# Hymba encoder layer: Hyena's projection begun ahead of the attention loop, and four small tables loaded by GpSimd at the start

## The chip, the cores and the metric

The kernel runs on one core of one Trainium2 chip. The metric is the device time of one execution in microseconds (us). Each core has a tensor engine (PE, with its weight loads shown apart as PEld), a vector engine (DVE), a scalar engine (ACT), GpSimd (POOL) and SyncE (SP), which issues most DMAs here. Each engine runs its instructions in the order of its own queue; between engines and DMAs they wait on semaphores.

## What is computed

One encoder layer on x of 2048 tokens by 1024 features, float32. A root-mean-square norm and one input projection give q (8 heads of 64), k and v (2 heads of 64), and u (3 x 512 columns). Half of the mixer is grouped-query attention over all tokens, half is a Hyena operator on u: a convolution of width 3, then two rounds of a long convolution by FFT with filters from a small network, each gated. Then output projection, residual, MLP, residual, norm. Cut to the lines that matter here:

```
proj = rms_norm(x, norm1_g) @ w_in
q, k, v, u = split(proj)                  # 512, 128, 128, 1536 columns
att = softmax(q k^T / 8) v                # after norm and rotation of q and k
v, x1, x2 = split(short_conv(u, conv_w, conv_b))      # 3 taps per column
z = v; for n, gate in ((0, x1), (1, x2)): z = gate * (fft_long_conv(z, taps_f[n]) + skip_d[n] * z)
taps = (h @ w4) * exp(-t * abs(deltas))   # h from a small network on time features; taps_f is their FFT
mix = concat(rms_norm(att), rms_norm(z)); h = x + mix @ w_out; MLP; norm
```

## The kernel before

All matrices stay float32: an operand is split into a high and a low part, and `mm3` (lines 162 to 166) makes a product of three matmuls. Stage 1, `qkv_proj`, takes 16 tiles of 128 tokens: transposes of the normed x (`tp`), 8 x 3 matmuls each for two groups of columns (`qkv`), norm and rotation on DVE and POOL, then transposes of the result (`tq`), a cast on ACT into `qs` (three buffers) and stores by SP of `q_d`, `k_d` and `v_d`. The split input weights of q, k and v (`wh`, `wl`) stay in SBUF for the whole stage. The normed, split x is stored too (`aT_d`), for u. `filter_hidden` runs beside it (`sx`, `hc`).

Attention has 32 units (16 query blocks for each of the two key heads) of 16 steps. A step makes one score peak (`sc` on PE, `top` on DVE), one block of weights (`st`, two matmuls, then the exponential `p` on ACT), sums of p on POOL (`sum`), and products with v (`o`, later `of`). Peaks run 22 steps ahead of the weights (`AHEAD`). At each step one yield of side work is taken: first 16 yields of `taps_ahead`, with an empty one after each (`spaced`), so 8 taps, then one yield of taps for every six of `u_proj` (`mixed`), and what remains runs behind the loop. Taps are `ft` (two matmuls), `taps` on DVE and a store to `taps_d`.

`u_proj` computes u and the short convolution: four blocks of 512 tokens by 12 column tiles of 128. For the first block, a column tile's weights are loaded (`uraw`), split on ACT and DVE in eight pieces (`uw`, lines 361 and 363), and stored (`uw_d`) for the other blocks, the split of the next tile running beside the matmuls (`uo`, 24 a tile) of this one. Its first yields are the nine of the first weight tile; each column tile has ten more. The order in attention and stage 1 is found by the framework's scheduler from the dependencies and the order of the code; each engine's queue is then fixed. From `filter_dft` on (`fs` on line 1465) the order is that of the code. SP's DMAs have eight semaphore lanes in turn, so that a DMA waits for the one eight places ahead to land.

The small tables are the convolution's weights and bias `cw` and `cb` (4608 and 1536 elements), the filters' decays `dl` (2048) and the skip weights `skip` (1024). They are loaded one 4-byte element at a time, by SP, at the start of attention: lines 336 and 339 in `u_proj`, 1278 and 1286 in `taps_ahead`.

Of the kernel before, what the change touches and what calls it, by code (L numbers as in the profile page):

```python
# [11 lines left out]
F32 = mybir.dt.float32  # L12
F32R = mybir.dt.float32r
# [32 lines left out]
def setup(tc, ctx, a):  # L46
# [10 lines left out]
    aligned(k.cpool, 64)  # L57
# [114 lines left out]
def qkv_proj(k, pa, ps, side):  # L172
# [10 lines left out]
    nc.gpsimd.memset(unit[:, 0:1], 1.0)  # L183
    W = QW + 2 * NKV * HD
    wh = pa.tile([P, ND, W], F32R, name="wh", bufs=1)
    wl = pa.tile([P, ND, W], F32R, name="wl", bufs=1)

    def load_w(c0, c1):
        for d in range(ND):
            raw = pa.tile([P, c1 - c0], F32, name=f"wraw{c0}", bufs=2)  # L190
# [5 lines left out]
    def load_x(t):  # L196
        xt = pa.tile([P, DM], F32, name="xt", bufs=2)
        nc.sync.dma_start(out=xt[:], in_=x[t * P:(t + 1) * P, :])
        return xt
# [99 lines left out]
    for i in range(-1 - XL, NT + FL):  # L299
# [21 lines left out]
        if 0 <= i < NT:  # L321
            okv = project(*aT.pop(i), QW, 256)
        if 0 <= i - 1 < NT:
            hl[i - 1] = twice(norm_rope(i - 1, *yz.pop(i - 1)))
        if 0 <= i < NT:
            yz[i] = taken(i, oq.pop(i), okv)
    pump(side, 10 ** 6)


def u_proj(k, pu, ps):  # L330
# [7 lines left out]
    cb = pu.tile([P, nct], F32, name="cb", bufs=1)  # L338
    nc.sync.dma_start(out=cb[:], in_=a["hy_conv_b"][0].rearrange("(c p) -> p c", p=P),
                      allow_slow_non_contiguous=True)  # L340
    edge = pu.tile([P, nct, 2], F32, name="edge", bufs=1)
    aligned(pu, 64)

    def load_a(b, d):
        t = pu.tile([P, 2, H], F32R, name="aT", bufs=ND)
# [3 lines left out]
    def load_w(b, ct):  # L349

        w = pu.tile([P, 2, ND, P], F32R, name="uw", bufs=2)
# [4 lines left out]
        raw = pu.tile([P, ND, P], F32, name="uraw", bufs=2)  # L356
# [16 lines left out]

    nw, rest = load_w(0, 0)
    aT = [load_a(0, d) for d in range(ND)]
    for _ in rest:
        yield
    for b in range(NB):
        last = b == NB - 1
        for ct in range(nct):  # L380
# [64 lines left out]
def attention(k, a1, ps, side):  # L445
# [94 lines left out]
    pump(side, START)  # L540
    for step in range(-AHEAD, total + FIN + 1):
# [34 lines left out]
START = 0  # L576
# [690 lines left out]
def filter_taps(k, f1, ps):  # L1267
# [535 lines left out]
```

## Time and profile before

| what | us |
|---|---|
| median of 3 runs | 3157.62 (3154.59 to 3162.08) |
| the profiled execution | 3165.88 |
| its span | 3164.1, mean granted clock 0.975 |
| stage 1, to its last transposes | 0 to 227.5 |
| attention, first `st` to the last `of` | 267.5 to 1219.6 |
| first `fs` behind attention | 1236.6 |

The rows that the prediction rests on follow the change. In them L with a number is a line of the kernel before; SPq, ACTq and the like are an engine's queue, where its DMAs are issued; a row of a timeline with a count stands for several instructions in a row.

### The profile page before, as it was taken

How to read it: one execution, taken by the hardware profiler on the slowest of the kernel's cores; microseconds unless marked ns; L12 is line 12 of the kernel's file. 1: busy time of each engine (PE TensorE's matmuls, PEld its weight loads, DVE VectorE, ACT ScalarE, POOL GpSimd, SP SyncE). 2: the span in 40 equal slices, each digit the busy share in tenths (PEclk: the TensorE clock that was granted, in tenths of full speed). 3: DMA queues.
4: the chain of work that ended last, by engine and by line, in shares of the span. 5: the costliest groups of instructions: out<-in, count | busy, mean ns of one | idle time of the engine just before them, and what ended most of it. 6: DMA issues, size and time to landing. Idle time of an engine off the chain costs nothing.

```text
span 3164.1 us, 40514 instructions
## 1 busy us (share of the span) xinstructions
PE 2989.5 (94%) x13400; PEld 2251.3 (71%) x13400; DVE 2048.8 (65%) x3153; ACT 1423.2 (45%) x2626; POOL 1715.1 (54%) x1399
## 2 busy tenths in 40 slices
PE   8978999999998998999999988999999989999998
PEld 6755666666665666676667766888788778888887
DVE  7987777666665554777465567778877535454455
ACT  7866655555553444444444563333433223223333
POOL 3434777778776876244555326777876635250010
PEclk9988999999998999999999998999999999999999
DMA  7758334324334425776656784445644395333454
GB/s 226 221 155 232 115 125 159 110 95 151 125 107 108 140 80 163 263 248 218 186 172 197 253 290 157 156 154 174 204 158 151 121 316 171 133 115 129 146 181 153
DMA packets 482462, 534.45 MB, mean 169 GB/s; under 512 B 49604, under 2 KB 344004, under 8 KB 475212
## 3 DMA queue, kind: packets, MB, share of 16 engines
q1 hardware_dynamic: 464540, 513.16, 50.4%
q0 software_dynamic: 4480, 14.68, 1.3%
q10 hardware_dynamic: 13232, 4.01, 0.6%
q8 instruction: 107, 1.75, 0.2%
q14 instruction: 103, 0.84, 0.1%
HBM read 326.22 MB, written 198.19 MB: 166 GB/s over the span
## 4 chain that ended last, share of the span: by engine, by line
PE 75%; DVE 5%; DMA 5%; issue 3%; POOL 3%; ACT 2%; SPq 1%; ACTq 0%; POOLq 0%; DVEq 0%
PE o L502 7%; PE y L164 6%; PE y L165 6%; PE y L166 6%; PE g L166 5%; PE g L165 5%; PE g L164 5%; PE st L481 4%; PE X L1435 4%; PE st L482 3%; PE sc L461 3%; PE uo L164 3%; PE uo L165 2%; PE uo L166 2%; PE b L1565 2%
## 5 line engine op out<-in xcount | busy, mean ns | idle before, releaser
L489 POOL TENSOR_TENSOR sum<-sum,p 128x512 f32<-128x512 f32 x416 | 552.9, 1329 | 125.3 <-ACT p L484 98.9
L464 DVE TENSOR_REDUCE top<-sc 128x1 f32<-128x512 f32 x512 | 347.4, 687 | 255.4 <-PE sc L461 252.3
L484 ACT ACTIVATE p<-st 128x512 f32<-128x512 f32 x512 | 303.2, 597 | 317.6 <-PE st L482 299.9
L164 PE MATMUL g<-mh,wop 128*128 128x512 f32 x896 | 350.5, 391 | 17.9 <-ACT wop L914 17.6
L165 PE MATMUL g<-ml,wop 128*128 128x512 f32 x896 | 350.6, 391 | 2.8 <-DVE ml L925 2.8
L166 PE MATMUL g<-mh,wop 128*128 128x512 f32 x896 | 350.4, 391 | 2.4 <-DVE wop L915 2.4
L164 PE MATMUL y<-bh,ah 128*128 128x512 f32 x768 | 299.8, 391 | 15.5 <-ACT bh L1082 15.5
L1091 DVE TENSOR_TENSOR ah<-ar,ah 128x1024 fp32r<-128x1024 f32 x111 | 148.9, 1342 | 235.2 <-ACT ah L1090 232.9
L165 PE MATMUL y<-bh,ah 128*128 128x512 f32 x768 | 299.7, 390 | 0.0
L166 PE MATMUL y<-bh,ah 128*128 128x512 f32 x768 | 299.7, 390 | 0.0
L1090 ACT CAST ah<-ar 128x1024 fp32r<-128x1024 f32 x111 | 117.0, 1054 | 347.8 <-PE y L166 343.0
L502 PE MATMUL o<-p,vt 128*64 128x512 f32 x1024 | 234.9, 598 | 0.0
L461 PE MATMUL sc<-kt,q 128*128 128x512 f32 x512 | 208.0, 410 | 15.0 <-DVE top L464 11.9
L481 PE MATMUL st<-q,kt 128*128 128x512 f32 x512 | 215.0, 420 | 1.6 <-ACT p L484 1.4
L164 PEld LDWEIGHTS g<-mh,wop 128*128 128x128 f32 x896 | 169.2, 189 | 54.2 <-ACT wop L914 18.0
L482 PE MATMUL st<-q,kt 128*128 128x512 f32 x512 | 203.8, 398 | 0.0
L165 PEld LDWEIGHTS g<-ml,wop 128*128 128x128 f32 x896 | 169.0, 189 | 38.9 <-DVE ml L925 3.9
L166 PEld LDWEIGHTS g<-mh,wop 128*128 128x128 f32 x896 | 169.1, 189 | 38.4 <-DVE wop L915 3.5
L914 ACT CAST wop<-ws 128x512 fp32r<-128x512 f32 x128 | 79.1, 621 | 223.5 <-PE g L166 192.1
L164 PEld LDWEIGHTS y<-bh,ah 128*128 128x128 f32 x768 | 144.7, 189 | 46.2 <-ACT bh L1082 15.9
L166 PEld LDWEIGHTS y<-bh,ah 128*128 128x128 f32 x768 | 144.7, 188 | 30.3
L165 PEld LDWEIGHTS y<-bh,ah 128*128 128x128 f32 x768 | 144.7, 188 | 30.2 <-DVE bh L1083 0.2
(306 smaller groups left out, 7054.6 us busy)
## 6 DMA issues: line engine op xcount, KB each, us to landing
ar<-H_d SPq DMA_DIRECT2D x111, 512.0 KB, 3.8
uw<-uw_d SPq DMA_DIRECT2D x36, 1024.0 KB, 5.0
w1raw<-in_w_mlp_in SPq DMA_DIRECT2D x64, 512.0 KB, 4.2
H_d<-r SPq DMA_DIRECT2D x96, 256.0 KB, 2.2
H_d<-s SPq DMA_DIRECT2D x96, 256.0 KB, 2.0
F_d<-F SPq DMA_DIRECT2D x34, 512.0 KB, 3.2
F<-F_d SPq DMA_DIRECT2D x34, 512.0 KB, 4.6
aT<-aT_d SPq DMA_DIRECT2D x32, 512.0 KB, 6.6
```

The source lines that it names most:

```text
L164: mm(out, l_hi, r_hi, start=start, stop=False)
L165: mm(out, l_hi, r_lo, start=False, stop=False)
L166: mm(out, l_lo, r_hi, start=False, stop=stop)
L461: nc.tensor.matmul(s[:], u.q[:, h], kt[u.kv, b][0][:], start=True, stop=True)
L464: nc.vector.tensor_reduce(out=u.top[:, h, b:b + 1], in_=s[:], axis=AX.X, op=ALU.max, negate=True)
L481: nc.tensor.matmul(s[:], lo[:, c], u.q2[:].rearrange("p h t -> p (h t)"), start=True, stop=False)
L482: nc.tensor.matmul(s[:], hi[:, c], u.q[:].rearrange("p h t -> p (h t)"), start=False, stop=True)
L484: nc.scalar.activation(out=p[:], in_=s[:], func=AF.Exp)
L489: nc.gpsimd.tensor_add(out=u.sum[:], in0=u.p0[:] if j == 1 else u.sum[:], in1=p[:])
L502: nc.tensor.matmul(u.o[cols], vt[j // 8][:, j % 8, u.kv], p[:], start=j < 2, stop=j > 13)
L1091: nc.vector.tensor_sub(out=h[:, 1], in0=raw[:], in1=f32(h[:, 0]))
L1435: k.nc.tensor.matmul(d[:, ri], t[:, m], Af[:, 2 * j + at], start=True, stop=True)
```

## The change

The weights `wh` and `wl` get a pool of their own, which ends behind the last tile's matmuls. In its memory `u_proj` is begun there: its first weight tile and the eight `aT` loads of its first block are issued. When attention begins, 49 yields of u are taken ahead of all else: nine for the first weight tile, and four column tiles. The peak of step 12 of the first unit may not be issued before the last of these matmuls. The four small tables are loaded by GpSimd at the kernel's start, behind the memsets of `unit`, and kept for the whole kernel. Stage 1's pools move to the other side of the memory.

```diff
@@ setup: the four small tables get places in the constant pool
     k.norm = k.cpool.tile([P, 4], F32, name="norm")
-    aligned(k.cpool, 64)
+    k.cw = k.cpool.tile([P, 3, 12], F32, name="cw")
+    k.cb = k.cpool.tile([P, 12], F32, name="cb")
+    k.dl = k.cpool.tile([P, 16], F32, name="dl")
+    k.skip = k.cpool.tile([P, 2, 4], F32, name="skip")
+    aligned(k.cpool, 256)
@@ mm3
-    mm(out, l_lo, r_hi, start=False, stop=stop)
+    return mm(out, l_lo, r_hi, start=False, stop=stop)
@@ qkv_proj: the tables' loads, the weights' own pool, and its early end
-def qkv_proj(k, pa, ps, side):
+def qkv_proj(k, pa, ps, side, after):
     nc.gpsimd.memset(unit[:, 0:1], 1.0)
+    nc.gpsimd.dma_start(out=k.cw[:], in_=a["hy_conv_w"][0].rearrange("w (c p) -> p w c", p=P),
+                        allow_slow_non_contiguous=True)
...
+    pw_pool = sbuf(k, "pw")
+    pw = pw_pool.__enter__()
+    wh = pw.tile([P, ND, W], F32R, name="wh", bufs=1)
+    wl = pw.tile([P, ND, W], F32R, name="wl", bufs=1)
...
             okv = project(*aT.pop(i), QW, 256)
+            if i == NT - 1:
+                pw_pool.__exit__(None, None, None)
+                next(after())
@@ u_proj
-def u_proj(k, pu, ps):
+def u_proj(k, pu):
-    cw = pu.tile([P, 3, nct], F32, name="cw", bufs=1)
-    nc.sync.dma_start(out=cw[:], in_=a["hy_conv_w"][0].rearrange("w (c p) -> p w c", p=P),
-                      allow_slow_non_contiguous=True)
...
+    cw, cb = k.cw, k.cb
+    held = [pu.tile([P, 2, H], F32R, name="aT", bufs=ND)]
+    held += [pu.tile([P, 2, ND, P], F32R, name="uw", bufs=2), pu.tile([P, ND, P], F32, name="uraw", bufs=2)]
...
     nw, rest = load_w(0, 0)
     aT = [load_a(0, d) for d in range(ND)]
+    yield
...
-                mm3(k, o[:], wh[:, d], wl[:, d], aT[d][:, 0], aT[d][:, 1], d == 0, d == ND - 1)
+                k.mark_u = mm3(k, o[:], wh[:, d], wl[:, d], aT[d][:, 0], aT[d][:, 1], d == 0, d == ND - 1)
@@ attention
-        nc.tensor.matmul(s[:], u.q[:, h], kt[u.kv, b][0][:], start=True, stop=True)
+        with k.tc.issue_after(behind) if len(units) == 1 and i == 12 else nullcontext():
+            nc.tensor.matmul(s[:], u.q[:, h], kt[u.kv, b][0][:], start=True, stop=True)
...
     pump(side, START)
+    behind = k.mark_u.ins
...
-START = 0
+START = 9 + 40
@@ taps_ahead
-    dl = f1.tile([P, 16], F32, name="dl")
-    nc.sync.dma_start(out=dl[:], in_=a["filt_deltas"][0].rearrange("(c p) -> p c", p=P),
-                      allow_slow_non_contiguous=True)
+    dl, skip = k.dl, k.skip
...
-    skip = f1.tile([P, 2, 4], F32, name="skip")
-    nc.sync.dma_start(out=skip[:], in_=a["hy_skip_d"][0].rearrange("o (c p) -> p o c", p=P),
-                      allow_slow_non_contiguous=True)
@@ encoder_layer
-            with sbuf(k, "p1", 2) as p1, sbuf(k, "f1") as f1:
+            def u_ahead():
+                k.up = sbuf(k, "up")
+                k.u = u_proj(k, k.up.__enter__())
+                return k.u
+
+            with sbuf(k, "p1", 2, side="right") as p1, sbuf(k, "f1", side="right") as f1:
...
-                    attention(k, at, ps, chain(islice(spaced(taps, 1), 16), mixed(taps, MA, u_proj(k, up, ps), MB)))
+                    side = chain(islice(k.u, START), islice(spaced(taps, 1), 16), mixed(taps, MA, k.u, MB))
+                    attention(k, at, k.ps, side)
```

(The loads of cb, dl and skip have the same form as that of cw. `edge` and the alignments move as well.)

On SP at the end of stage 1, before, the last tiles' stores are followed by the small tables:

```order
L287 DMA k_d<-qs 128x4x128
L287 DMA q_d<-qs 128x4x128 x2
L287 DMA k_d<-qs 128x4x128
L287 DMA q_d<-qs 128x4x128 x2
L287 DMA k_d<-qs 128x4x128
L1278 DMA dl<-in_filt_deltas 128x16x1
L1286 DMA skip<-in_hy_skip_d 128x8x1
L1292 DMA tr<-in_trow 128x512
L422 DMA kt<-k_d 128x512 x4
L441 DMA vt<-v_d 128x8x128
L1292 DMA tr<-in_trow 128x512
L336 DMA cw<-in_hy_conv_w 128x36x1
```

Now the loads of u stand ahead of the last stores, and the store of split weights (`uw_d`) between them (lines of the changed kernel here and below: L301 and L251 are the stores of before's L287 and L237):

```order
L301 DMA k_d<-qs 128x4x128
L375 DMA uraw<-in_w_in 128x8x128
L364 DMA aT<-aT_d 128x2x512 x8
L251 DMA v_d<-v 128x128
L301 DMA q_d<-qs 128x4x128 x2
L301 DMA k_d<-qs 128x4x128
L387 DMA uw_d<-uw 128x2048
L301 DMA q_d<-qs 128x4x128 x2
L301 DMA k_d<-qs 128x4x128
L375 DMA uraw<-in_w_in 128x8x128
L301 DMA q_d<-qs 128x4x128 x2
L301 DMA k_d<-qs 128x4x128
```

So nine loads of 512 KB moved ahead of the stores of the last three tiles, and the four tables left.

On PE at the end of stage 1, before, the last transposes are followed at once by peaks and taps:

```order
L279 MATMUL tq<-identr,kk 128x128 x4
L279 MATMUL tq<-identr,hl 128x128 x8
L279 MATMUL tq<-identr,kk 128x128 x4
L461 MATMUL sc<-kt,q 128x512 x6
L1301 MATMUL ft<-hc,w4h 128x512 x2
L461 MATMUL sc<-kt,q 128x512
L1301 MATMUL ft<-hc,w4l 128x512 x2
L461 MATMUL sc<-kt,q 128x512 x6
L1301 MATMUL ft<-hc,w4h 128x512
L1301 MATMUL ft<-hc,w4l 128x512
```

Now 96 `uo` stand between the last transposes and the first peak (the three dots leave out `uo` rows alone):

```order
L293 MATMUL tq<-identr,kk 128x128 x4
L168 MATMUL uo<-aT,uw 128x512
L169 MATMUL uo<-aT,uw 128x512
L170 MATMUL uo<-aT,uw 128x512
...
L170 MATMUL uo<-aT,uw 128x512
L483 MATMUL sc<-kt,q 128x512
L1319 MATMUL ft<-hc,w4h 128x512
L1319 MATMUL ft<-hc,w4l 128x512
L483 MATMUL sc<-kt,q 128x512 x2
L1319 MATMUL ft<-hc,w4h 128x512
L1319 MATMUL ft<-hc,w4l 128x512
L483 MATMUL sc<-kt,q 128x512 x13
```

Up to the first `st` there are 21 `sc` in both, with ten pairs of `ft` before and six now. On POOL the DMA of cw now stands ahead of the select that finishes `ident`, and those of cb, dl and skip behind it.

On PE at the end of attention, before, `uo` are the last rows ahead of the next stage's `fs`:

```order
L166 MATMUL uo<-aT,uw 128x512
L164 MATMUL uo<-aT,uw 128x512
L165 MATMUL uo<-aT,uw 128x512
L166 MATMUL uo<-aT,uw 128x512
L1465 MATMUL fs<-table,e 128x128 x108
L645 MATMUL at<-ident,mx 128x128 x4
```

Now the products of attention's last unit are:

```order
L504 MATMUL st<-q,kt 128x512
L503 MATMUL st<-q_10883,kt 128x512
L504 MATMUL st<-q,kt 128x512
L524 MATMUL o<-p,vt 64x512 x5
L535 MATMUL of<-fold,ob 128x65 x4
L1483 MATMUL fs<-table,e 128x128 x108
L668 MATMUL at<-ident,mx 128x128 x4
```

The last `uo` moved from behind attention to ahead of its last steps.

## Rows read from the trace of the kernel before

**Rows 1.** The page: part 1 (busy us, share of the span, instructions of the engines) and the first line of part 4 (the chain of work that ended last, by engine).

```profile
PE 2989.5 (94%) x13400; PEld 2251.3 (71%) x13400; DVE 2048.8 (65%) x3153; ACT 1423.2 (45%) x2626; POOL 1715.1 (54%) x1399
...
PE 75%; DVE 5%; DMA 5%; issue 3%; POOL 3%; ACT 2%; SPq 1%; ACTq 0%; POOLq 0%; DVEq 0%
```

**Rows 2.** Windows of 10 us around the end of stage 1 and the start of attention. Columns: window, its length, busy us and instructions of each engine (PE, PEld, DVE, ACT, POOL), granted TensorE clock, DMA share, GB/s.

```profile
210.00:220.00 10.00, 4.88 (x21) 2.26 (x21) 9.80 (x19) 7.00 (x15) 4.52 (x5) 0.91 0.37 111
...
230.00:240.00 10.00, 3.15 (x6) 1.96 (x7) 5.19 (x15) 1.33 (x3) 0.00 (x0) 0.50 0.89 200
240.00:250.00 10.00, 5.40 (x11) 2.54 (x10) 6.15 (x12) 4.37 (x7) 0.00 (x0) 0.67 0.96 148
250.00:260.00 10.00, 6.12 (x13) 3.10 (x12) 5.43 (x14) 6.44 (x17) 0.00 (x0) 0.54 0.94 281
...
270.00:280.00 10.00, 10.00 (x41) 7.02 (x39) 7.68 (x15) 7.11 (x15) 9.18 (x7) 1.00 1.03 359
```

**Rows 3.** The chain of waits through the same stretch, in order of time: start us, us, what it was.

```profile
229.60 4.05 DMA k_d<-qs
...
237.08 4.64 DMA kt<-k_d
241.74 6.65 SPq L339
...
248.50 4.95 DMA uraw<-in_w_in
```

**Rows 4.** Timelines of POOL, PE, ACT and SP at the end of attention: start us, us (of all of the row's instructions), engine, line, operation, out<-in, count, and in brackets the idle time before it and what ended it.

```profile
1195.31 18.46 POOL L489 TENSOR_TENSOR sum<-sum,p 128x512 f32<-128x512 f32 x13
...
1219.57 1.11 PE L513 MATMUL of<-fold,ob 128*128 128x65 f32 x8 [0.72 <-POOL ob L507]
...
1225.07 12.24 ACTq L619 DMA_DIRECT2D n<-n_d  x7
...
1236.18 0.39 PE L165 MATMUL uo<-aT,uw 128*128 128x512 f32 x1
1236.41 0.39 PE L166 MATMUL uo<-aT,uw 128*128 128x512 f32 x1
1236.64 1.05 PE L1465 MATMUL fs<-table,e 128*128 128x128 f32 x8
...
1240.45 2.12 SPq L414 DMA_DIRECT2D u_d<-uy  x2
...
1246.29 15.56 SPq L1381 DMA_DIRECT2D x<-taps_d  x11
```

**Rows 5.** The DMAs of 228 to 250 us: packets and bytes, then the queue of SP's DMAs with packets, MB and its share of the 16 engines' time.

```profile
DMA packets 13285, 3.97 MB, mean 181 GB/s; under 512 B 9438, under 2 KB 12005, under 8 KB 13285
...
q1 hardware_dynamic: 12645, 2.92, 73.7%
```

**Rows 6.** Windows of 2 us at the start of the kernel, columns as in rows 2.

```profile
6.00:8.00 2.00, 0.00 (x0) 0.00 (x0) 0.89 (x2) 1.43 (x3) 0.00 (x0) 1.00 0.97 371
8.00:10.00 2.00, 0.00 (x0) 0.00 (x0) 1.61 (x9) 1.72 (x4) 0.00 (x0) 1.00 0.68 193
...
18.00:20.00 2.00, 1.72 (x6) 0.96 (x6) 1.74 (x3) 2.00 (x4) 0.00 (x0) 1.00 1.13 347
```

**Rows 7.** Timeline of the first 12 us, the rows of `ident` on POOL and DVE and PE's first transposes.

```profile
1.20 0.29 POOL masks.py:199 TENSOR_SCALAR_AFFINE_SELECT ident<-ident 128x128 f32<-128x128 f32 x1
...
9.10 0.22 DVE L55 CAST identr<-ident 128x128 fp32r<-128x128 f32 x1
...
11.41 0.87 PE L215 MATMUL tp<-ident,xs 128*128 128x128 f32 x3 [11.41 <-ACT xs L206]
```

**Rows 8.** POOL's own DMAs in the kernel before: their queue in part 3 of the page (packets, MB, share), and one form of line 799 (duration on POOL in ns, min/median/max, first and last start).

```profile
q0 software_dynamic: 4480, 14.68, 1.3%
...
L799 POOL DMA_DIRECT2D ml<-sa x8: 536/536/714, 1783.0 to 1831.5; - x8
```

**Rows 9.** Timelines of SP, ACT and PE at the end of stage 1, columns as in rows 4.

```profile
211.13 0.36 SPq L287 DMA_DIRECT2D k_d<-qs  x1
...
213.12 0.91 SPq L287 DMA_DIRECT2D q_d<-qs  x2
...
219.20 1.05 ACT L281 CAST qs<-tq 128x512 fp32r<-128x512 f32 x2
...
227.49 0.72 PE L279 MATMUL tq<-identr,kk 128*128 128x128 f32 x4 [0.26 <-ACT qs L281]
```

**Rows 10.** Timelines of DVE and PE from the first score peak to the first `st`, columns as in rows 4.

```profile
231.63 0.69 DVE L464 TENSOR_REDUCE top<-sc 128x1 f32<-128x512 f32 x1
...
240.58 1.89 DVE L464 TENSOR_REDUCE top<-sc 128x1 f32<-128x512 f32 x3
...
267.48 0.63 PE L481 MATMUL st<-q,kt 128*128 128x512 f32 x1
267.91 0.63 PE L482 MATMUL st<-q,kt 128*128 128x512 f32 x1
```

**Rows 11.** Groups of instructions from 268 to 630 us by line and shape: busy us, mean ns of one, idle us before them and what ended it.

```profile
L363 DVE SCALAR_TENSOR_TENSOR uw<-uraw,g,uw 128x128 fp32r<-128x128 f32 x94 | 57.9, 661 | 2.2 <-ACT uw L361 2.2
```

**Rows 12.** Two windows of 250 us inside attention, columns as in rows 2.

```profile
300.00:550.00 250.00, 238.22 (x1028) 156.65 (x1025) 180.44 (x309) 147.38 (x307) 180.91 (x138) 0.98 0.42 134
550.00:800.00 250.00, 249.92 (x1109) 167.65 (x1108) 158.66 (x245) 137.07 (x251) 197.74 (x149) 1.00 0.38 125
```

More of the change, by code (lines that the diff above doesn't have):

```diff
@@ L1 @@
 import math
-from contextlib import ExitStack
+from contextlib import ExitStack, nullcontext
 from itertools import chain, islice
@@ L183, in qkv_proj @@
     nc.gpsimd.memset(unit[:, 0:1], 1.0)
+    nc.gpsimd.dma_start(out=k.cw[:], in_=a["hy_conv_w"][0].rearrange("w (c p) -> p w c", p=P),
+                        allow_slow_non_contiguous=True)
+    nc.gpsimd.dma_start(out=k.cb[:], in_=a["hy_conv_b"][0].rearrange("(c p) -> p c", p=P),
+                        allow_slow_non_contiguous=True)
+    nc.gpsimd.dma_start(out=k.dl[:], in_=a["filt_deltas"][0].rearrange("(c p) -> p c", p=P),
+                        allow_slow_non_contiguous=True)
+    nc.gpsimd.dma_start(out=k.skip[:], in_=a["hy_skip_d"][0].rearrange("o (c p) -> p o c", p=P),
+                        allow_slow_non_contiguous=True)
     W = QW + 2 * NKV * HD
[L185 to L186 removed]
+    pw_pool = sbuf(k, "pw")
+    pw = pw_pool.__enter__()
+    wh = pw.tile([P, ND, W], F32R, name="wh", bufs=1)
+    wl = pw.tile([P, ND, W], F32R, name="wl", bufs=1)
     def load_w(c0, c1):
         for d in range(ND):
[L190 removed]
+            raw = pw.tile([P, c1 - c0], F32, name=f"wraw{c0}", bufs=2)
             nc.sync.dma_start(out=raw[:], in_=w_in[d * P:(d + 1) * P, c0:c1])
@@ L196, in load_x @@
     def load_x(t):
-        xt = pa.tile([P, DM], F32, name="xt", bufs=2)
+        xt = pw.tile([P, DM], F32, name="xt", bufs=2)
         nc.sync.dma_start(out=xt[:], in_=x[t * P:(t + 1) * P, :])
@@ L334, in u_proj, with first @@
     H, NB = 512, 4
-    cw = pu.tile([P, 3, nct], F32, name="cw", bufs=1)
-    nc.sync.dma_start(out=cw[:], in_=a["hy_conv_w"][0].rearrange("w (c p) -> p w c", p=P),
-                      allow_slow_non_contiguous=True)
-    cb = pu.tile([P, nct], F32, name="cb", bufs=1)
-    nc.sync.dma_start(out=cb[:], in_=a["hy_conv_b"][0].rearrange("(c p) -> p c", p=P),
-                      allow_slow_non_contiguous=True)
-    edge = pu.tile([P, nct, 2], F32, name="edge", bufs=1)
-    aligned(pu, 64)
+    cw, cb = k.cw, k.cb
+    held = [pu.tile([P, 2, H], F32R, name="aT", bufs=ND)]
+    held += [pu.tile([P, 2, ND, P], F32R, name="uw", bufs=2), pu.tile([P, ND, P], F32, name="uraw", bufs=2)]
+    def first(i, *args, **kw):
+        t, held[i] = held[i], None
+        return t or pu.tile(*args, **kw)
     def load_a(b, d):
-        t = pu.tile([P, 2, H], F32R, name="aT", bufs=ND)
+        t = first(0, [P, 2, H], F32R, name="aT", bufs=ND)
         nc.sync.dma_start(out=f32(t[:]), in_=k.aT_d[:, d * P:(d + 1) * P, b * H:(b + 1) * H].rearrange("a p t -> p a t"))
@@ L349, in load_w @@
     def load_w(b, ct):
-        w = pu.tile([P, 2, ND, P], F32R, name="uw", bufs=2)
+        w = first(1, [P, 2, ND, P], F32R, name="uw", bufs=2)
         if b:
@@ L355, in load_w @@
         c0 = 768 + ct * P
-        raw = pu.tile([P, ND, P], F32, name="uraw", bufs=2)
+        raw = first(2, [P, ND, P], F32, name="uraw", bufs=2)
         nc.sync.dma_start(out=raw[:], in_=w_in[:, c0:c0 + P].rearrange("(d p) c -> p d c", p=P))
@@ L372, in load_w @@
         return w, split()
+    edge = pu.tile([P, nct, 2], F32, name="edge", bufs=1)
+    aligned(pu, 160)
     nw, rest = load_w(0, 0)
     aT = [load_a(0, d) for d in range(ND)]
+    yield
     for _ in rest:
```

13 lines of the change are left out of this document (7 added, 6 removed).

## The prediction

> **What bounds the kernel now.** I read the page's first parts, then the windows of the stretches that the diff touches, then the chain of waits through them, then the timelines there. The page says that PE is busy for 94% of the span and that 75% of the chain that ended last is PE [rows 1]. So a change can pay only in three ways: less PE work (there is none of it here, the same matmuls run), a hole of PE filled, or a tail cut off. The windows show the hole: from 210 to 260 us PE is busy between 3.15 and 6.12 of every 10 us, from 230 at a granted clock of 0.50 to 0.67 (0.50 is the 1.2 GHz level), with a DMA share of 0.89 to 0.96 [rows 2]. The chain through the hole is a row of transfers: the last k_d store 4.05, kt 4.64, SP's issue of cb 6.65, then uraw 4.95 [rows 3]. The second place is the end of attention: the last `of` of attention starts at 1219.57 us and the first `fs` of the next stage at 1236.64, and between them PE runs nothing but u's projection, 72 matmuls [rows 4].
>
> The profiled execution took 3165.88 us (span 3164.1), 8.3 above the median of 3157.62. The differences below are worked out on the profiled one and taken off the median.
>
> **The change part by part.**
>
> *The small tables leave the hole.* They are 4608 + 1536 + 2048 + 1024 = 9216 elements of 4 bytes, and of 13285 packets between 228 and 250 us 9438 are under 512 B: the tables are nearly all of them [rows 5]. That queue moved 2.92 MB in 22 us at 73.7% of the engines, 16.2 us; at some 300 GB/s (250 to 260 us shows 281 [rows 2]) the bytes want 9.7, so the small packets took about 6.5 us of all engines. Gone with them is SP's 6.65. This is in the times of the hole below.
>
> *The tables at the start.* The same 6.5 us of small packets now fall between 1 and 20 us, where the DMA share is already 0.68 to 1.13 [rows 6]. PE starts at 11.41 and is busy 1.72 of the 2 us from 18 to 20, so it has work while the loads run. If the packets delay every weight load, +6.5; if they slip beneath PE's work, 0. On POOL the DMA of cw now stands ahead of the select that makes `ident`. Before, that ran at 1.20 for 0.29, DVE's cast of it at 9.10, and PE's first transposes at 11.41 [rows 7]: 7.6 us of room. POOL's own DMAs take 536 ns each, and the 56 of them made 4480 packets, 80 each [rows 8]. At that price per DMA the ident is in time; at that price per packet 4608 elements take 58 x 0.536 = 31 us, and the start is 31 - 7.6 = 23 us late. I take +1, nearest to the row's price per DMA; the bounds are 0 and +23.
>
> The Trainium skill, "DMA: Bandwidth & Descriptors", section "Issuing engines are not separate DMA queues", speaks against this part: DMAs of SP, ACT and POOL end on the same 16 engines, and another issuer saves issue time alone. The DMA share there [rows 6] agrees with it, and by that rule the start costs the whole +6.5 and the sum would be 5.5 us higher (rival E below).
>
> *The hole.* In SP's order uraw and eight aT loads (9 x 0.5 MB, 4.7 MB) now stand behind the k_d store of 211.13 and ahead of the stores of the last tiles. At 281 to 359 GB/s [rows 2] that is 13 to 17 us, so they land by 225 to 228. The stores queued behind them land at 230 to 232, where those of the same tile went out at 213 to 214 before. `qs` has three buffers, so the casts of tile 14 wait for these stores (about 231, 219.2 before), and tile 15's for tile 14's, behind a 1 MB store of split weights too. The last transposes, before at 227.49 [rows 9], come at about 238.4: +11, between 0 (the stores slip in between) and +15. Who waits: PE, which has the 96 uo matmuls queued behind those transposes.
>
> Then 96 uo run. At full clock they come every 0.229 us (22.0 us; [rows 4], 1236.18 to 1236.41), at half clock every 0.43 (st at 267.48 and 267.91 [rows 10]). With some 5 us of half clock they take 24 us and end at 262.4. DVE's share of them fits: 0.66 us for each of 8 pieces of a weight tile [rows 11], 5.3 a tile against 5.5 of PE.
>
> Then all the score peaks are still to come, for no `sc` can be issued before PE has passed the uo: DVE needs 0.60 us a peak (1.89 for three [rows 10]), 12.6 for the 21, about 4 for six taps blocks, some 3 for weight pieces, low and diag. That is 20 us, and the first `st` is at 282 (276 to 289), against 267.48 [rows 10]: **+14.5**. The gain is not the hole's whole idle time, because the uo wait for the transposes and the peaks wait for the uo.
>
> Ten pairs of `ft` were done before the first `st`, now six: four pairs, 8 matmuls of 0.229, **+1.8**, go into the loop.
>
> *The start of the loop.* Between 300 and 550 us PE issues 1028 matmuls, between 550 and 800 1109 [rows 12]: 81 fewer, at 250/1109 us each 18 us lost while weight tiles are split on ACT and DVE. Five of the twelve tiles are now split before the loop: 18 x 5/12 = **-7** (0 to -12).
>
> *The end of attention.* One yield of side work goes with each step as before, so u, 49 yields ahead, ends some 18 steps before attention does, and the loop up to there is the same work. In the last 13 steps POOL's sums stand back to back, 18.46 us [rows 4]; without u these steps get no shorter, and the five ahead of them gain about 0.3 each: **-1**. Behind the last `of` the 72 matmuls are gone: 1236.64 - 1220.7 = 16 us. Two things move with them. ACT's seven loads of n, 12.24 us of issue [rows 4], now have no u ahead of them, but also no cover: ACT's copies of `fs` behind them start about 11 us earlier and not 16. The x loads at 1246.29, which feed the later `fs`, no longer stand behind the u_d stores of 1240.45 and may come 20 us earlier. I take **-16**, between -11 and -20.
>
> Sum: +1 + 14.5 + 1.8 - 7 - 1 - 16 = -6.7. From the median: 3157.6 - 6.7 = **3151 us**.
>
> **Rivals.**
>
> *A, the forecast*: the tail pays 16, the delay of attention eats most of it. 3151, own range 3145 to 3156.
>
> *B, even*: the stretch after the uo is worse than its count of DVE work. For: in the rows the same peaks and taps took 36 us, from 231.6 to 267.5 [rows 10], and the clock may fall again. Against: that stretch waited on transfers that are gone. With the first `st` at 289 it is +7: 3158.
>
> *C, slower*: POOL's descriptors for cw hold `ident`. Place: the start, the POOL row ahead of the select. Price: with 31 us for cw +23, by half of that +8; below the room of 7.6 nothing, so it decides from about 1.6 us a thousand elements on. For: the price per packet of POOL's DMAs, if packets are what costs. Against: they hold POOL for 0.54 only. 3151 - 1 + 8 to 23: 3158 to 3173, mostly above 3164.
>
> By the Trainium skill, "SBUF — State Buffer", the box on the "DVE blocks DMA" trap, POOL can't write descriptors while DVE runs some of its copies. POOL's DMAs at line 799 hold 536 ns in the median and 714 at the most [rows 8], so the trace shows little of it; at the start DVE is busy 2.5 of the 4 us from 6 to 10 [rows 6], and by that rule ident would be late by up to 2.5 and the sum 3153.5, inside A's range.
>
> *D, better*: the stores slip between the loads and the last transposes stay near 228, or the x loads bring the whole 20. First `st` at 272 to 275, 3140 to 3144.
>
> *E, even*: the 6.5 us of small packets, freed from the hole, delay the first weight loads by as much, 3156.5. For: the DMA share at the start [rows 6]. Against: PE has work while they run, 1.72 of the 2 us from 18 to 20.
>
> That u gains nothing since PE meets the 96 uo late adds to B alone; they stand ahead of every `sc`, so the tail is shorter in any case.
>
> **How the numbers follow.** A measurement of this kernel can tell about 0.2%, 6.3 us, from no change. Chances: A 0.38, B 0.18, C 0.17, D 0.16, E 0.11. A lies on both sides of 3151.3; with 0.28 of it beyond and D's 0.16 and a little of the rest, faster has 0.45; same takes A's other part and most of B and E, 0.36; slower has most of C and B's or E's with more than their price, 0.19. The range takes in D's 3140 and C's middle: 3138 to 3167.
>
> **What would show it.** Right: last transposes near 238, uo from there to about 262, first `st` near 282, no uo behind the last `of`, the first `fs` about a microsecond after it, PE's matmul count per 250 us up by some 30 in the first loop window. Wrong: `ident` cast after 9.1 with the first `tp` later than 12 (C); uo before 230 or first `st` before 276 (D); first `st` behind 287, or `fs` gaps of 10 us that wait for ACT or x (B). The sum rests most on the hole: every microsecond of the first `st` goes into the time one for one, as PE has no slack behind it.

## The result, and the profile after

The changed kernel takes 3141.72 us (median of 4, 3138.51 to 3143.60) against 3158.39 (median of 4, 3154.59 to 3162.08): a ratio of 0.9941, 95% interval 0.9928 to 0.9955, so 14 to 23 us less. (The quotient of these medians is 0.9947; the ratio, here and below, is the estimate on record.) The forecast was 3151. Its profiled execution took 3142.40, span 3140.6, which is 23.5 below the span of before; before's profiled run, 3165.88, lay 7.5 above its median. A second profile of before, taken later, has a span of 3160.4 and is used below where the first may be off.

The span divides at six points. The times are starts or ends in the traces; unit 8 is the 129th `p`, unit 24 the 385th, unit 26 the 417th; X is the first matmul of the next stage's second step.

| stretch | before | changed | difference | predicted |
|---|---|---|---|---|
| start to the last `qkv` | 209.2 | 213.7 | +4.5 | +1 |
| to the first `st` | 58.3 | 75.0 | +16.7 | +14.5 |
| to unit 8 | 247.6 | 239.4 | -8.2 | -5.2 (split stalls -7, taps +1.8) |
| units 8 to 24 | 458.0 | 454.4 | -3.6 | 0 |
| units 24 and 25 | 72.4 | 68.1 | -4.3 (-1.6 by the second profile) | 0 |
| unit 26 to the end of the last `of` | 175.2 | 171.4 | -3.8 | -1 |
| to X | 70.5 | 50.7 | -19.8 | -16 |
| X to the end | 1872.9 | 1867.9 | -5.0 | 0 |

At the start, the timeline of the changed kernel's POOL, DVE and PE (columns as in rows 4; L188 is the load of cw):

```profile
1.34 2.01 POOL L188 DMA_DIRECT2D cw<-in_hy_conv_w  x1 [0.31 <-issue]
...
3.44 0.30 POOL masks.py:199 TENSOR_SCALAR_AFFINE_SELECT ident<-ident 128x128 f32<-128x128 f32 x1
...
11.06 0.22 DVE L55 CAST identr<-ident 128x128 fp32r<-128x128 f32 x1
...
14.82 1.94 PE L229 MATMUL tp<-ident,xs 128*128 128x128 f32 x8 [14.82 <-ACT xs L220]
```

[rows 7] had the select at 1.20, the cast at 9.10 and `tp` at 11.41. POOL is held by cw for 2.01 us, not 31, and `ident` is ready at 3.74, seven us ahead of its first use; `tp` waits for ACT's `xs`, as before. So rival C's sign (a cast after 9.1 and `tp` later than 12) was seen without C's mechanism. The windows of 2 us at the same place (columns as in rows 2) show what was late:

```profile
8.00:10.00 2.00, 0.00 (x0) 0.00 (x0) 1.11 (x5) 0.19 (x1) 0.01 (x1) 1.00 1.32 57
10.00:12.00 2.00, 0.00 (x0) 0.00 (x0) 0.29 (x2) 0.95 (x2) 0.00 (x0) 1.00 1.42 87
12.00:14.00 2.00, 0.00 (x0) 0.00 (x0) 0.11 (x1) 1.37 (x3) 0.00 (x0) 1.00 1.18 128
```

At DMA shares of 1.18 to 1.42 only 57 to 128 GB/s are moved; [rows 6] had 0.68 at 193 GB/s in the first of these windows. The tables' packets share the engines with the weight loads: from 1 to 14 us, 256 KB of `wraw` land 7.2 us after their issue (the median), 3.6 before.

The stretch up to the first `st`, in windows of 10 us:

```profile
220.00:230.00 10.00, 1.70 (x2) 0.30 (x2) 9.94 (x25) 8.15 (x16) 0.52 (x2) 0.63 0.94 300
230.00:240.00 10.00, 2.17 (x12) 1.69 (x12) 5.33 (x14) 3.01 (x5) 0.40 (x1) 0.50 0.96 339
240.00:250.00 10.00, 8.61 (x30) 7.07 (x31) 3.21 (x15) 4.42 (x12) 0.00 (x0) 0.68 1.00 288
250.00:260.00 10.00, 10.00 (x45) 8.27 (x45) 6.57 (x17) 6.02 (x15) 0.00 (x0) 1.00 1.05 365
...
270.00:280.00 10.00, 8.28 (x15) 4.21 (x15) 8.83 (x18) 1.94 (x3) 0.00 (x0) 0.52 0.95 295
280.00:290.00 10.00, 7.37 (x16) 4.15 (x15) 7.47 (x18) 9.30 (x26) 0.00 (x0) 0.50 0.92 312
```

Beside [rows 2] the DMA rates stand out: 288 to 365 GB/s where before had 148 to 281. The DMAs of 212 to 290 us (as rows 5):

```profile
DMA packets 20756, 23.06 MB, mean 296 GB/s; under 512 B 975, under 2 KB 15311, under 8 KB 20111
...
q1 hardware_dynamic: 20111, 21.96, 86.6%
```

23.06 MB in 78 us (before, 10.75 MB from 212 to 268 us), where the prediction counted 4.7 MB of new loads. It left out six more weight tiles of 0.5 MB (`uraw`) and, but for one, the stores of 1 MB that follow them (five `uw_d` fall in here). The chain of waits has transfers at both ends of the uo (as rows 3):

```profile
227.20 8.63 DMA q_d<-qs
...
236.52 4.04 DMA q_d<-qs
...
268.71 8.38 DMA tr<-in_trow
```

PE's timeline shows the last `tq` of stage 1 and the first `st`:

```profile
241.39 0.72 PE L293 MATMUL tq<-identr,kk 128*128 128x128 f32 x4 [2.59 <-ACT qs L295]
...
288.66 0.63 PE L503 MATMUL st<-q,kt 128*128 128x512 f32 x1
```

The last `tq` at 241.39 is the predicted 238.4 and the late start; the 96 uo take 24.0 us from 241.91 to the first `sc` that follows them at 265.9, as predicted; the 22.7 us from there to the first `st` are 2.7 more than predicted. In them `ex`, which the taps need, waits for `tr` until 277, and the granted clock is 0.52 and 0.50 in the last two windows (0.50 is the 1.2 GHz level).

Inside attention, as rows 12:

```profile
300.00:550.00 250.00, 243.46 (x1067) 162.45 (x1066) 175.48 (x294) 145.78 (x291) 191.33 (x144) 0.99 0.40 135
```

PE issues 39 more matmuls in this window than in [rows 12]; the prediction had some 30. At the end of attention, timelines of ACT, PE and SP (as rows 4):

```profile
1212.93 0.52 ACTq L642 DMA_DIRECT2D n<-n_d  x1
...
1216.04 6.02 ACTq L642 DMA_DIRECT2D n<-n_d  x5
...
1220.06 1.97 PE L535 MATMUL of<-fold,ob 128*128 128x65 f32 x8 [5.51 <-POOL ob L529]
...
1221.82 6.73 PE L1483 MATMUL fs<-table,e 128*128 128x128 f32 x40
...
1223.10 2.99 SPq L616 DMA_DIRECT2D oraw<-in_w_out  x4
...
1223.87 0.58 ACT L1436 COPY A<-fs 64x512 f32<-64x512 f32 x1 [8.05 <-DMA n<-n_d]
...
1227.62 16.28 SPq L1399 DMA_DIRECT2D x<-taps_d  x12
```

The `fs` start 1221.82, right behind the last `of`. All eight n loads are issued by 1222.06, and their issue begins 7.1 us ahead of that `of`, where [rows 4] has them from 1225 to 1237.3; oraw and the x loads follow, the latter at 1227.62, 7.6 us behind the `of` and not 26.7 (1246.29 - 1219.57).

### The profile page after: what moved, and what is told of

The parts are those of the page before. It is cut to its first block, busy times and chain, and to the rows that moved or that the text cites. A ratio compares the mean times of both kernels' runs of the same rounds, so it can differ in the third digit from the quotient of the medians.

```text
span 3140.6 us, 40519 instructions
## 1 busy us (share of the span) xinstructions
PE 2979.8 (95%) x13400; PEld 2250.3 (72%) x13400; DVE 2033.9 (65%) x3153; ACT 1424.6 (45%) x2626; POOL 1717.2 (55%) x1403
## 3 DMA queue, kind: packets, MB, share of 16 engines
q1 hardware_dynamic: 455260, 513.12, 50.0%
q0 software_dynamic: 4704, 14.72, 1.4%
## 4 chain that ended last, share of the span: by engine, by line
PE 77%; DVE 4%; DMA 4%; issue 3%; POOL 2%; ACT 2%; SPq 0%; ACTq 0%; POOLq 0%; DVEq 0%
PE o L524 7%; PE y L168 7%; PE y L170 6%; PE y L169 6%; PE g L170 6%; PE g L169 6%; PE g L168 6%; PE st L503 4%; PE X L1453 4%; PE st L504 4%; PE sc L483 3%; PE uo L168 3%; PE uo L169 3%; PE uo L170 3%; PE b L1583 2%
## 5 line engine op out<-in xcount | busy, mean ns | idle before, releaser
L1114 DVE TENSOR_TENSOR ah<-ar,ah 128x1024 fp32r<-128x1024 f32 x111 | 147.2, 1326 | 236.8 <-ACT ah L1113 236.7
```

Source lines behind the costliest of these rows:

```text
L1114: nc.vector.tensor_sub(out=h[:, 1], in0=raw[:], in1=f32(h[:, 0]))
```

## The experiments

Ratios are to runs of the kernel before on the same chip. "Changed" is the changed kernel, from which the edits start unless the text says otherwise.

| kernel | ratio, 95% interval | last `qkv` | first `st` | unit 8 | last `of` ends | from there to X |
|---|---|---|---|---|---|---|
| before (first, second profile) | 1 | 209.2, 209.9 | 267.5, 269.0 | 515.1, 514.9 | 1220.7, 1217.8 | 70.5, 70.4 |
| changed | 0.9941 (0.9928 to 0.9955) | 213.7 | 288.7 | 528.1 | 1222.0 | 50.7 |
| tables_only | 0.9989 (0.9980 to 0.9997) | 213.0 | 268.5 | 513.7 | 1216.1 | 69.8 |
| u_hole | 0.9951 (0.9938 to 0.9963) | 207.9 | 294.2 | 528.4 | 1223.8 | 49.3 |
| tables_later | 0.9936 (0.9923 to 0.9950) | 209.2 | 286.1 | 528.4 | 1222.1 | 49.9 |
| loads_late | 0.9959 (0.9947 to 0.9971) | 212.0 | 288.9 | 531.2 | 1225.6 | 50.4 |
| up_first | 1.0008 (1.0000 to 1.0017) | 209.9 | 265.6 | 508.8 | 1212.1 | 76.9 |
| start9 | 0.9976 (0.9967 to 0.9986) | 214.0 | 278.0 | 515.5 | 1210.8 | 70.5 |
| start29 | 0.9969 (0.9958 to 0.9979) | 214.1 | 283.9 | 516.4 | 1214.5 | 64.2 |
| start29_later | 0.9969 (0.9959 to 0.9980) | 208.1 | 279.1 | 518.0 | 1217.3 | 63.8 |
| start34 | 0.9942 (0.9929 to 0.9954) | 214.6 | 289.1 | 520.5 | 1212.1 | 58.6 |
| start39 | 0.9942 (0.9929 to 0.9956) | 214.0 | 292.8 | 525.3 | 1221.2 | 51.9 |
| start89 | 0.9961 (0.9949 to 0.9973) | 212.2 | 313.3 | 545.0 | 1227.3 | 52.0 |

**before_again.** The kernel before, unchanged, run once.

> The kernel before, unchanged, for a second profile. The profiled runs differ by 23.5 us, the medians by 16.7: units 8 to 24 of attention run the same instructions in both and yet take 28.6 us each before and 28.4 in the changed kernel, and the stages behind the first X add another 5 us. Theory 1 (the profiled run of before was a slow one, nothing of the change is in these places): about 3157, units of 28.4 to 28.5 and the stretch from the first X to the end about 1848 to 1850 us long. Theory 2 (the change works there too, by placement): units of 28.6 again and 1873 us as in the first profile.

3162.43 us. Units 8 to 24 took 458.0 again, X to the end 1872.2, as Theory 2 had it. So units 8 to 24 do differ by 3.6 us between the two kernels (windows of both, then of up_first below); only the stall in units 24 and 25 (69.7 here) was longer in the first profile by chance.

**tables_only.** The kernel before with the changed kernel's table loads, u not ahead.

```
+    nc.gpsimd.dma_start(out=k.cw[:], ...)   # cb, dl, skip alike, behind the memsets of unit
-    nc.sync.dma_start(out=cw[:], ...)       # in u_proj and taps_ahead, cb, dl, skip alike
```

> Only the small tables move to POOL at the start; u is not ahead. Theory 1 (their packets delay the first weight loads): last qkv matmul 4.4 us later than before, the identr cast not the cause; the hole gets shorter by the 6.5 us of packets and SP's 6.65 us, so the first st at 262 to 266; net -1 to -6, 3152 to 3157. Rival (the start is delayed by ident waiting behind cw on POOL): the first tp starts right behind ident's cast. Rival (the tables cost nothing in the hole): first st at 272, net +4.4, 3162.

3158.20 against 3161.10, ratio 0.9989: -3 us. PE's first transposes (as rows 4); POOL's rows of cw and the select are those of the changed kernel above:

```profile
15.51 1.94 PE L227 MATMUL tp<-ident,xs 128*128 128x128 f32 x8 [15.51 <-ACT xs L218]
```

`ident` was ready at 3.74 and `tp` came at 15.51: so POOL was not what delayed it, and the packets are what is left (tables_later, below, moves them and loses the delay). The hole became shorter by 3.6 us (59.1 to 55.5 from the last `qkv` to the first `st`, before's second profile and here), and the start longer by 3.1. The first `st` at 268.5 misses the 262 to 266 expected: 6.5 us of packets and SP's 6.65 us of issue were not paid back in full. The tables alone are worth some 3 us.

**u_hole.** u ahead, but the tables loaded by SP behind the last store of stage 1.

```
-    nc.gpsimd.dma_start(out=k.cw[:], ...)           # and cb, dl, skip
+    with k.tc.issue_after(k.mark_s.ins):            # the last store of qs on SP
+        k.nc.sync.dma_start(out=k.cw[:], ...)       # cb here, dl and skip in taps_ahead
```

> The changed kernel, but the tables loaded by SP behind the last store of stage 1, about where they were before. Theory 1 (packets at the start cost 4.4, in the hole some 6 to 10, since the uo matmuls cover part): last qkv at 209, the first st 288 to 294, total 3141 to 3148. Rival (the uo cover the tables' packets wholly, so the move to POOL was a loss): first st about 284, total 3137.

3145.27, ratio 0.9951. PE's first `st`:

```profile
294.15 0.40 PE L495 MATMUL st<-q,kt 128*128 128x512 f32 x1
```

That is as Theory 1 had it, first `st` and total. The first `st` is 5.5 us behind the changed kernel's, and yet unit 8 begins at 528.4 against 528.1; the ratios' intervals overlap.

**tables_later.** POOL issues the tables behind its work on tile 3.

```
+    if i == 4:
+        with k.tc.issue_after(k.mark_p.ins):        # a product of tile 3 on POOL
+            nc.gpsimd.dma_start(out=k.cw[:], ...)   # and cb, dl, skip
```

> The changed kernel, but POOL issues the tables behind its work on tile 3 of stage 1, some 50 us in, when the DMA share is 0.3 to 0.5. Theory 1 (packets against the first loads): the 4.4 us come back, last qkv at 209 to 210, total 3136 to 3138. Rival (the small packets delay whatever load they meet, here x tiles and stores): last qkv 212 to 214, total 3141 to 3143.

3141.72, ratio 0.9936. The last `qkv` and the first `st`:

```profile
208.93 0.28 PE L170 MATMUL qkv<-wh,al 128*128 128x256 f32 x1
...
286.05 0.63 PE L505 MATMUL st<-q,kt 128*128 128x512 f32 x1
```

The tables went out from 65.4 us on, later than expected. The start's delay is gone (the last `qkv` ends at 209.2, as before). At the first `st` 2.6 us of it are left, at unit 3 (the 49th `p`) none: 386.3 against 386.1. The rival of this run is refuted by the last `qkv`, but the 3136 to 3138 expected were not had: the total is that of the changed kernel within the intervals.

**loads_late.** u's loads written behind the last tile's stores.

```
-                next(after())                  # at the last tile's matmuls
+    next(after())                              # behind the loop over the tiles
```

> The changed kernel, but u's loads are written behind the last tile's stores, and the scheduler puts the aT loads between and behind the stores. Theory 1 (the stores behind 4.7 MB of loads hold the last transposes, and with them the uo; but a head start of a few us is lost again in the first units): last tq at 231 to 234 instead of 242, first uo at 236 to 240, first st 281 to 286, total within 2 us of the changed kernel. Rival (one for one): total 4 to 7 us below the changed kernel.

3147.62, ratio 0.9959: by the ratios some 5 us slower than the changed kernel (the intervals overlap slightly), outside both expectations. PE's last `tq`, first uo and first `st`, then the DMAs of 212 to 290 us, then two transfers of the chain of waits:

```profile
231.18 0.72 PE L293 MATMUL tq<-identr,kk 128*128 128x128 f32 x4 [0.26 <-ACT qs L295]
...
231.70 0.76 PE L168 MATMUL uo<-aT,uw 128*128 128x512 f32 x1
...
288.89 0.63 PE L503 MATMUL st<-q,kt 128*128 128x512 f32 x1
```

```profile
DMA packets 20078, 21.83 MB, mean 280 GB/s; under 512 B 898, under 2 KB 15234, under 8 KB 19433
```

```profile
235.09 9.23 DMA aT<-aT_d
...
250.97 6.51 DMA uraw<-in_w_in
```

The transposes came 10.2 us sooner, as both theories had it, and the first `st` not at all: 288.89 against 288.66. The same stretch moved 21.83 MB at 280 GB/s. So the stores behind the loads are what held the transposes, and not what held the first `st`: the uo, which came sooner, waited for their own loads instead. That the bytes alone set the length of this stretch is not shown; with fewer tiles ahead the first `st` does not come sooner in even steps (278.0 with START 9, 283.9 with 29, 289.1 with 34, 292.8 with 39, 288.7 with 49). Why the loop then ran 3 us later is not settled.

**up_first.** The kernel before, u's pool below attention's in SBUF, every instruction in the same place of its queue.

```
-            with sbuf(k, "at") as at, sbuf(k, "up") as up:
+            with sbuf(k, "up") as up, sbuf(k, "at") as at:
```

> The kernel before with the same instructions in the same order on every engine; only u's pool lies below attention's in SBUF, as in the changed kernel, and not above it. In attention's units 8 to 24 the changed kernel takes 454.4 us and before 458.0, with the same matmuls and PE busy throughout; uo follow each other after 228.5 ns there and after 231.8 before. Theory 1 (placement of the operands makes the difference): 228 to 229 ns here, units 8 to 24 in 454 to 455, total 5 to 8 us below before. Theory 2 (it goes with how the side work is offset against the steps, 49 yields ahead): 231.8 ns and 458 us as before, total as before within 3.

3161.42, ratio 1.0008. (Its loop ran 6 us ahead of before's, and its tail took 6.5 us longer, 76.9.) The windows of units 8 to 24 of the changed kernel, of before (second profile), and of this one:

```profile
528.10:982.50 454.40, 454.20 (x2026) 304.43 (x2025) 289.30 (x453) 250.07 (x457) 360.92 (x272) 1.00 0.38 126
```

```profile
514.90:972.90 458.00, 457.46 (x2026) 304.88 (x2025) 291.54 (x450) 249.54 (x458) 361.17 (x273) 1.00 0.38 125
```

```profile
508.80:966.50 457.70, 457.24 (x2026) 304.86 (x2025) 292.31 (x450) 249.64 (x458) 360.95 (x273) 1.00 0.38 125
```

The same 2026 matmuls, PE busy throughout, take 454.4, 458.0 and 457.7 us; from uo to uo, on average, 228.6 ns in the changed kernel, 231.7 and 231.8 in the two others. That u's pool lies below attention's is not the cause. Not tried is the order inside that pool, where the changed kernel has `aT`, `uw` and `uraw` first and no cw and cb.

**start9.** u's loads and first weight tile ahead, no column tile.

```
-START = 9 + 40
+START = 9          # without issue_after at step 12
```

> The changed kernel with START 9: u's first loads and its first weight tile are ahead, no uo is made to precede the peaks. Theory 1 (the tail behind attention is what pays; the delay of the first st is largely taken up in the first units, which are not bound by PE alone): first st about 270, some 40 uo and u's copies behind the last of again, total 3147 to 3153. Rival (the delay of the first st costs one for one, as the prediction had it, so that giving up both cancels): 3139 to 3144.

3153.94, ratio 0.9976: far from the rival, and 1 us above Theory 1's range, whose tail came as expected; the first `st`, at 278.0, came later than its 270. The loop is 11 us ahead of the changed kernel's at the last `of`, and the tail is long again: ACT, PE and SP at the end of attention:

```profile
1209.67 1.10 PE L534 MATMUL of<-fold,ob 128*128 128x65 f32 x8 [0.73 <-POOL ob L528]
...
1220.66 0.59 ACT L421 COPY u<-uo 128x512 f32<-128x512 f32 x1 [4.01 <-PE uo L170]
...
1222.26 12.97 ACTq L640 DMA_DIRECT2D n<-n_d  x8
...
1224.46 8.89 SPq L614 DMA_DIRECT2D oraw<-in_w_out  x4
...
1236.18 16.66 SPq L1397 DMA_DIRECT2D x<-taps_d  x12
```

uo run 10 us behind the `of`, until 1220.6, and X comes 20 us later than with 49. The copy of the last u stands ahead of the n loads on ACT; these need 12.97 us of issue, oraw 8.89 at the same time, and the x loads come at 1236.18, 26.5 us behind the `of`; before had 26.7.

**start89.** Eight column tiles ahead.

```
-START = 9 + 40
+START = 9 + 80
```

> The changed kernel with START 89: eight column tiles ahead instead of four. Theory 1 (the tail is gone already with 49, PE has work through the loop, and the last 36 steps without u are bound by POOL's sums at 1.42 us): first st near 312, total 3144 to 3150. Rival (every tile taken out of the loop saves split stalls worth more): 3136 to 3140.

3148.38, ratio 0.9961, as Theory 1 had it. Unit 8 is 16.9 us later than with 49, from unit 26 to the last `of` 12 are won back, the tail stays at 52.

**start29, start34, start29_later, start39.** The number of yields ahead is 29, 34, 29 with the tables as in tables_later, and 39.

> The changed kernel with START 29: two column tiles ahead, 48 uo before the first st, and by the order the last uo stand one row ahead of attention's last of. Theory (the traffic of the stretch before the first st, 23 MB at near the engines' full share, sets its length, so fewer tiles ahead make it shorter by about 6 us at unit 8; the tail's gain hangs on u's last copies and on the n loads being issued before the last of): unit 8 at 521 to 523; if the tail is as short as with 49 (51 us from the last of to X) total 5 us below the changed kernel, about 3136; if the n loads stay behind u's copies (70 us with START 9) 10 to 14 above it. Rival (uo matmuls behind the last of are all that the tail costs): tail of 52 to 55, total 3138 to 3141.

> The changed kernel with START 34: 2.5 column tiles ahead, last uo nine rows ahead of the last of. All variants so far with 228 ns between uo in units 8 to 24 were 9 yields past a whole number of tiles ahead, before (232 ns) was not. Theory 1 (the offset of the side work against the steps decides): 230 to 232 ns and 457 to 459 us for units 8 to 24 here. Theory 2 (something else of the changed code): 228 and 454 to 455. On the tail: 51 to 56 us from the last of to X, total 3137 to 3142.

> START 29 and the small tables issued by POOL behind tile 3 of stage 1. Theory (a head start in stage 1 is lost in the first units): the last qkv 4 us earlier than with START 29 alone, unit 8 within 1.5 us of it, total within 2. Rival (with the shorter hole the head start comes through): 3 to 4 us below START 29.

> The changed kernel with START 39: three column tiles ahead. Theory (two slopes: each tile less ahead brings unit 8 some 3 to 4 us sooner, and the tail from the last of to X stays near 51 us as long as the last u copy leaves ACT in time to issue the n loads before the last of): unit 8 at 522 to 525, tail 51 to 55, total 1 to 4 us below START 49. Rival (the tail grows from 49 down in even steps, 58.6 with START 34): tail 55 to 57, total as with 49 and 34, within 1.5 us.

start29 took 3148.15 (0.9969), start34 3138.55 (0.9942), start29_later 3150.15 (0.9969), start39 3143.50 (0.9942). With 29 unit 8 came at 516.4, sooner than the 521 to 523 expected; the uo end ahead of the last `of`, and the tail is still 64.2 us. Its end of attention:

```profile
1213.43 1.11 PE L535 MATMUL of<-fold,ob 128*128 128x65 f32 x8 [1.86 <-POOL ob L529]
...
1213.59 16.48 ACTq L642 DMA_DIRECT2D n<-n_d  x8
...
1229.30 17.43 SPq L1399 DMA_DIRECT2D x<-taps_d  x12
```

The n loads start only at the `of` and hold ACT for 16.48 us. The x loads stand on SP behind oraw, whose issue takes 8.7 us beside them (2.99 with 49), and come 15.9 us after the `of`. So the rival of that run, that the matmuls behind the last `of` are the tail's whole cost, falls. With 34 the tail was expected at 51 to 56 and took 58.6. Its ACT and PE there:

```profile
1208.35 12.06 ACTq L642 DMA_DIRECT2D n<-n_d  x8
...
1224.36 7.20 PE L1483 MATMUL fs<-table,e 128*128 128x128 f32 x48 [6.65 <-ACT A L1438]
```

u's last copy had left ACT 9 us ahead of the last `of` (1210.36), the n loads were begun 2 us ahead of it, and PE still waited 6.65 us for ACT's copies behind them.

With 34 the uo follow each other after 228.7 ns too, so this offset of the side work against the steps does not bring back the 231.8. The pace of the uo is not all that units 8 to 24 depend on: with it they took 456.7 us with 34, 458.8 with 29 (where PE waits 2.4 us for a load of `kt`) and 459.9 in start29_later. start29_later is start29 within the intervals, though its last `qkv` ended 6.0 us sooner, as its theory had it. start39 had the unit 8 (525.3) and the tail (51.9) of its theory, and the total of its rival. From 34 to 49 the ratios are flat: what the loop wins by fewer tiles ahead (unit 8 at 520.5, 525.3, 528.1), the tail gives back (58.6, 51.9, 50.7). No version beats the changed kernel beyond the intervals, though by the medians start34 would stand at 0.9929; whether it is a few us faster stays open.

## Why the prediction was right in its sign and 9 us short

**The end of attention: -16 predicted, -19.8 measured, for another reason than the 72 matmuls.** The step took u's matmuls as the price and the n and x loads as a correction to it between -11 and -20. The START series shows the order of the two: with 10 us of uo behind the `of` the tail is as long as with 16, and with none (29) it is 64.2, 6 us less. The rest goes with the n loads: their issue ends 0.0, 1.3, 2.2, 8.3, 15.5 and 24.5 us behind the end of the last `of` with START 49, 39, 89, 34, 29 and 9, and the tail is 50.7, 51.9, 52.0, 58.6, 64.2 and 70.5. With 9 and 29 u's last copy stands right ahead of them on ACT; with 34 it does not, and their issue is slow all the same. No run moved the n loads alone, so that they set the tail is argued from this order. With 49 the x loads follow the `of` by 7.6 us: the extreme of -20, named with the x loads as its reason, came out.

**The hole: +14.5 predicted, +16.7 measured.** Transposes and uo came as forecast, behind the late start. The 20 us of peaks and taps, worked out from DVE's time, were 22.7; the stretch moved 23.06 MB and waited for `tr`. The step left out the next weight tiles and all but one of the 1 MB stores that the uo bring with them. So the first `st`, at 288.7, met rival B's sign (behind 287), and B's time of 3158 did not follow.

**The start: +1 predicted, +4.5 measured.** Rival E's mechanism, nearer to its 6.5 than to 1: tables_only has the delay, tables_later has not. Rival C did not come about, cw held POOL for 2.01 us. The Trainium skill's rule on issuing engines ("DMA: Bandwidth & Descriptors", section "Issuing engines are not separate DMA queues"), by which another issuing engine saves issue time alone, agrees with the first, the last `qkv` at +4.5; of the "DVE blocks DMA" trap ("SBUF — State Buffer") these rows show nothing, as DVE was busy for 0.15 of the 4 us from 2 to 6 in which POOL issued most of the tables.

**The step that failed: "every microsecond of the first `st` goes into the time one for one, as PE has no slack behind it".** First `st` at 286.1, 288.7 and 294.2 (tables_later, changed, u_hole) give unit 8 at 528.4, 528.1 and 528.4; the three stand together from unit 3 on (386.3, 386.1 and 386.4). start29_later's head start at the last `qkv` is lost in the same way. PE does have slack in the first units: it waits for DVE there, which stands in weight splits. Timelines of DVE and PE in the changed kernel:

```profile
324.76 6.14 DVE L381 SCALAR_TENSOR_TENSOR uw<-uraw,g,uw 128x128 fp32r<-128x128 f32 x7
...
331.65 1.58 PE L535 MATMUL of<-fold,ob 128*128 128x65 f32 x7 [3.40 <-DVE u L411]
```

Seven pieces of a split take DVE 6.14 us, and PE waits 3.40 for the DVE row behind them. But this wait is as long in the other two (3.39 in tables_later, where the `of` starts at 329.04, and 3.38 in u_hole, at 333.53), and so is the next, of 2.90 us near 380. What differs is the clock behind the waits. Windows of 4 us of tables_later, of the changed kernel and of u_hole (columns as in rows 2):

```profile
332.00:336.00 4.00, 4.00 (x11) 3.03 (x11) 1.64 (x3) 1.16 (x2) 2.01 (x2) 0.51 0.63 184
...
380.00:384.00 4.00, 4.00 (x11) 3.14 (x10) 1.06 (x2) 2.00 (x5) 1.28 (x1) 0.53 0.90 258
```

```profile
332.00:336.00 4.00, 4.00 (x15) 3.49 (x15) 2.01 (x5) 0.60 (x1) 0.76 (x1) 0.60 0.99 286
...
380.00:384.00 4.00, 4.00 (x12) 3.17 (x12) 1.57 (x4) 2.53 (x5) 1.28 (x1) 0.62 0.97 267
```

```profile
332.00:336.00 4.00, 2.47 (x12) 2.18 (x13) 3.38 (x8) 0.55 (x1) 0.63 (x1) 0.84 0.67 215
...
380.00:384.00 4.00, 3.47 (x15) 2.86 (x16) 3.12 (x7) 2.24 (x5) 0.19 (x1) 1.00 0.87 260
```

By the granted clock, the windows from 328 to 340 and from 376 to 388 us lose 6.8 us of full speed in tables_later, 3.4 in the changed kernel and 1.7 in u_hole. An estimate from these: tables_later gives back 3.4 us against the changed kernel, and u_hole gains 1.7. Between the 17th and the 49th `p` they gave back 2.9 and gained 1.5; u_hole's other 3.6 us were gone by the 17th. Why the clock fell for longer in the earlier kernel was not tried. That the three meet within 0.3 us is in part luck: loads_late and start39 come out 3 us later and 3 us earlier at unit 8.

Nor does this step alone explain the 9 us. At unit 8 the changed kernel stands 13.0 us behind before, and 10.3 were forecast: what was missed was won behind it.

**The rest of the loop.** To unit 8 -8.2 for -5.2: the reason (fewer tiles left to split) is not borne out as a price by the tile: from the first `p` to unit 8 before took 246.5 us (244.9 in its second profile), and the START series 236.8 with 9, 231.6 with 29, 230.5 with 34, 231.8 with 39, 236.9 with 49 and 229.7 with 89. All are shorter than before, without an order by the tiles ahead, so the share of 5/12 was no good measure; half-clock stretches like those above differ between these kernels too. Units 8 to 24, -3.6, not predicted: the uo follow each other 1.4% faster in every variant of the changed kernel and in none of before. In the two largest groups of matmuls behind attention (`g`, `y`) the step from one to the next is 226.7 ns in both kernels, so the difference lies in attention alone. The order of the two pools and the offset tried with 34 are excluded; the cause stays open. The last units, -3.8 for -1, have no uo left. X to the end, -5.0: the same code, and the 14 profiles spread from 1866.0 to 1872.9. The two of before and tables_only are the highest, but up_first, also before's code, has 1869.2 and loads_late, the changed kernel's, 1871.5; that it belongs to the change is not shown.

The sum of the predicted terms was -6.7, the profiles give -23.5 and the medians -16.7. The range held, by rival D's 3140 to 3144, of which the half on the x loads came true and the half on an early first `st` did not. Of E's price of 5.5 us, 3.5 were paid at the start and did not reach the end.

## What to carry to other kernels

Don't carry a delay at a loop's start into the total one for one: three kernels whose loops began up to 8 us apart stood together again by the fourth unit, the earlier ones having run longer at half clock behind waits of the same length. At a change of stage, look for what is queued behind the last side work on the engine that issues the next stage's loads; moving that work off the end paid 20 us there, of which some 6 (START 29) came with its own 16 us of matmuls. Count all bytes that a step pulled forward brings with it, and what the transfer engines have left there: an order that brought the last transposes 10 us sooner brought the first `st` no sooner.

## What the runs showed of the hardware

POOL issued 4608 single elements (cw) in 2.01 us, 1536 in 1.06, 2048 in 1.15 and 1024 in 0.88, and its queue counted 4704 packets in all against 4480 before, 224 more for 9216 elements; SP's queue counted 464540 packets before and 455260 in the changed kernel, 9280 fewer. Beside these transfers the DMA engines moved 57 to 128 GB/s for about 6 us, at shares of 1.18 to 1.42. A matmul of 512 columns at the full granted clock followed the one before after 228.6 or 231.8 ns, in the same stretch of two kernels, by a cause that these runs did not find. And after waits of PE of the same length (3.4 us) at the same instructions, the clock granted in the 4 us from 332 on was 0.51, 0.60 and 0.84 in three kernels.
